# A hybrid attention layer: half-height score products tied into runs, the linear attention's levels taken two at a time

## The chip, the cores and the metric

One core of one Trainium2 chip runs the whole layer. The metric is the device time of one execution in microseconds (us), lower is better. The core has TensorE (products, with weights loaded ahead of them), VectorE, ScalarE, GpSimd and SyncE (which issues most of the transfers).

## What is computed

One layer over 256 latent tokens and 256 context tokens, width 2048, in float32. The part that the change touches:

```python
h = modulate(rms_norm(x, norm1_w), shift, scale)              # for latents and context
gq, gk, gv, gr, gaf, gab, dq, dk, dv = split(h @ w_in)
# linear attention, 8 heads of 64 (q, k) and 128 (v), forwards and backwards, with decays:
scores = einsum('bhid,bhjd,bhijd->bhij', qc, kc, exp(b_i - b_j))   # b: running sum of log decays
o = scores @ v + (q * exp(b)) @ state
# differential attention, 8 heads, two maps of 64 each, 256 queries, 512 keys:
q, k = rope(rms_norm(q)), rope(rms_norm(k))                   # k of the context without rope
p = softmax(q @ k.T * 64 ** -0.5)
o = (p[0] - lam * p[1]) @ v
# then: norms of o, gates, projections, output projection, gated MLP with a width-3 convolution
```

## The kernel before

The tokens lie in the free dimension, channels on the 128 partitions. Weights come from HBM in tiles of 512 KB, are split into a high and a low part (`split`: ScalarE copies to fp32r, L206; VectorE or GpSimd subtracts, L213), and each weights' product is made of two or three fp32r products over these parts (`col_tile` L262/L264, `row_tile` L275 to L277, `both_tile` L311 to L313). These products are the bulk of the time; the two attentions run between them.

The program is given to a planner that orders each engine's instructions by their priority and by its own simulated times; tiles of one tag share buffers, and a tile waits for a free one. Inside `high_priority(500)` an instruction goes ahead of the weights' products as soon as the planner thinks that its operands are there. `after(later, earlier)` ties two instructions of one engine in that order, without a wait. In PSUM there are four accumulator banks (`acc_bank`) and four auxiliary ones: two of the kind aux0, two of aux1 (`aux_bank(name, j)`).

The linear attention works on four pairs of heads (`gla_pair`), each pair's two heads on partitions 0 to 63 and 64 to 127. A pair makes its decays' running sums (`bfb`), the state from the context (key transposes L777, state products L782, both in aux0 banks), and then scores for two chunks of 128 tokens: one set for q and k as they are (`score(q, kl, ...)`), one off-diagonal set between the chunks, and one set for each of seven levels (`LEVELS`, spans of 64 down to 1). A level's factors `e` (two buffers) are four subtractions on GpSimd (L832 to L835), an exponential on ScalarE (L836) and a product with q and k on VectorE (L837). A set of scores is four f32 products of 64 rows (`score`, L808): two chunks, and in each the two heads, head j into a bank of kind aux j. Each bank is then copied into `at`: with a mask by VectorE for a level (L839), by ScalarE for the other two sets (L815, L822). At the end the outputs take two state products of 64 rows per head (L845) and two with values (L848).

The differential attention (`scores`, `attend`) takes 8 heads and two blocks of 128 queries. One `scores(h, c)` makes six fp32r products of 64 rows and 512 columns (L965): for each of the two maps m, on partitions m*64 to m*64+63 and into a bank of kind aux m, query high by key high, query low by key high, query high by key low. Per head the kind aux0 holds `s` twice, one `pT`, `o` and `oss`; the kind aux1 holds `s` twice and one `pT`. `halves` makes the high and low parts (high on ScalarE first, low on VectorE from it). The gates' products (`gate_tile`) and the projections (`pga`, `pgb`) follow.

The norms' sums (`sums`, 24 of them, in `heads_norm` and `onormed`) multiply a matrix of ones by the high and the low part of the squares (L594, L595).

Of the kernel before, what the change touches and what calls it, by code (L numbers as in the profile page):

```python
# [9 lines left out]
F32 = mybir.dt.float32  # L10
# [8 lines left out]
P = 128  # L19
D = 2048  # L20
T = 256
# [125 lines left out]
def layer_kernel(tc, I, out):  # L147
# [3 lines left out]
    with es:  # L151
# [438 lines left out]
        def sums(o, m, sq, halves=None):  # L590

            n = sq.shape[1]
            hi, lo = halves or split(sq, n)
            PE.matmul(o, m, hi[:, :n], start=True, stop=False)  # L594
            PE.matmul(o, m, lo[:, :n], start=False, stop=True)  # L595
# [77 lines left out]
        with tc.tile_pool(name="gla", bufs=1) as pg:  # L673
# [60 lines left out]
            def gla_pair(p):  # L734
# [67 lines left out]
                def score(Q, K, off, take):  # L802

                    bs = [aux_bank("sc", j) for j in range(2)]
                    for c in range(2):
                        cq = 1 - c if off else c
                        for j in range(2):
                            PE.matmul(bs[j][:, c * P:(c + 1) * P], K[j * 64:(j + 1) * 64, c * P:(c + 1) * P],  # L808
                                      Q[j * 64:(j + 1) * 64, cq * P:(cq + 1) * P], start=True, stop=True)
# [5 lines left out]
                score(q, kl, False, lambda v, b: S.activation(v, b, AF.Copy, scale=2.0))  # L815
                e = pg.tile([P, 2, T], F32, tag="e", bufs=2, name="e")
                S.activation(e[:, 0, P:], bfb[:, 0, P:], AF.Exp, scale=1.0 / 16)
                S.activation(e[:, 0, :P], bfb[:, 1, :P], AF.Exp, scale=1.0 / 16)
                S.activation(e[:, 1, :P], bfb[:, 0, :P], AF.Exp, scale=-1.0 / 16, bias=bl[:, 0:1])
                S.activation(e[:, 1, P:], bfb[:, 1, P:], AF.Exp, scale=-1.0 / 16, bias=bl[:, 1:2])  # L820
                V.tensor_tensor(e, e, qk[p][:, 0:2, :], op=ALU.mult)
                score(e[:, 0, :], e[:, 1, :], True, lambda v, b: S.copy(v, b))  # L822
                for li, m in enumerate(LEVELS):
                    e = pg.tile([P, 2, T], F32, tag="e", bufs=2, name="e")
                    g = T // (2 * m)
                    f4 = bfb[:, 0, :].rearrange("p (g h m) -> p g h m", h=2, m=m)
                    b4 = bfb[:, 1, :].rearrange("p (g h m) -> p g h m", h=2, m=m)
                    q4 = e[:, 0, :].rearrange("p (g h m) -> p g h m", h=2, m=m)
                    k4 = e[:, 1, :].rearrange("p (g h m) -> p g h m", h=2, m=m)
                    fm = f4[:, :, 0, m - 1:m].to_broadcast([P, g, m])  # L830
                    bm = b4[:, :, 1, 0:1].to_broadcast([P, g, m])
                    G.tensor_tensor(q4[:, :, 1, :], f4[:, :, 1, :], fm, op=ALU.subtract)  # L832
                    G.tensor_tensor(q4[:, :, 0, :], b4[:, :, 0, :], bm, op=ALU.subtract)
                    G.tensor_tensor(k4[:, :, 0, :], fm, f4[:, :, 0, :], op=ALU.subtract)
                    G.tensor_tensor(k4[:, :, 1, :], bm, b4[:, :, 1, :], op=ALU.subtract)  # L835
                    S.activation(e, e, AF.Exp, scale=1.0 / 16)  # L836
                    V.tensor_tensor(e, e, qk[p][:, 0:2, :], op=ALU.mult)  # L837
                    mk = masks[:, li:li + 1, :].to_broadcast([P, 2, P])
                    score(e[:, 0, :], e[:, 1, :], False, lambda v, b: V.copy_predicated(v, mk, b))  # L839
# [68 lines left out]
        with tc.tile_pool(name="diff", bufs=1) as pd:  # L908
# [49 lines left out]
            def scores(h, c):  # L958
# [3 lines left out]
                for i, j in ((0, 0), (1, 0), (0, 1)):  # L962
                    for m in range(2):
                        r = slice(m * 64, (m + 1) * 64)
                        PE.matmul(bs[m], qs[h][r, i, c * P:(c + 1) * P], ks[h][j][r, :], start=i + j == 0, stop=j == 1)  # L965
# [258 lines left out]
```

## Time and profile before

| | us |
|---|---|
| median of 3 runs | 1749.18 (1746.83 to 1751.12) |
| the profiled execution | 1749.72 |
| its span, first to last instruction | 1747.9 |
| TensorE busy | 1715.5 (98%), 10460 products |
| VectorE, ScalarE, GpSimd busy | 1230.4, 981.4, 491.8 |

The span lies inside the profiled execution's time; starts in the trace count from the span's start. In the trace's rows "L808 MATMUL sc<-e 64*128 64x128" is an instruction of line 808 that writes tile sc from tile e, with 64 rows and 128 columns of the array, and 64 partitions by 128 elements of moving operand. Neighbours of one line are merged (x8), and a merged row has the first one's start and the time to the last one's end; ends of products are modelled, starts are recorded. A bracket gives the idle time of the engine ahead of the row, and what ended it.

### The profile page before, as it was taken

The page shows a single profiled execution, that of the slowest core. Times are in us where ns is not written, and L with a number is a line of the kernel's source. Part 1 is how long each engine was busy: PE and PEld are TensorE (multiplying, and loading weights), DVE is VectorE, ACT ScalarE, POOL GpSimd, SP SyncE. Part 2 cuts the span into 40 slices and gives each one's busy share as a digit, 9 for nine tenths or more (in the row PEclk, how much of TensorE's full clock was granted, in tenths as well). Part 3 has the DMA queues.
Part 4 walks back from the last instruction along what each step waited for, and adds up shares of the span by engine and source line. Part 5 has one row for each costly group of instructions (what it writes and reads, how often), then busy time and mean ns, then how long its engine had stood idle before and what let it go on. Part 6 is the DMA issues. An engine that isn't in the chain of part 4 may idle for free. (4 is left out here: it accounts for less than half of the span.)

```text
span 1747.9 us, 29267 instructions
## 1 busy us (share of the span) xinstructions
PE 1715.5 (98%) x10460; PEld 1473.6 (84%) x10460; DVE 1230.4 (70%) x2230; ACT 981.4 (56%) x1980; POOL 491.8 (28%) x474
## 2 busy tenths in 40 slices
PE   8999999999999999999999999999999999999999
PEld 5779999988877788887878898888888888888888
DVE  4555756778687787767876888777877877644443
ACT  5335455664345776744655676666666666544443
POOL 0002534646121222223353422222222222222222
PEclk9999999999999999999999999999999999999999
DMA  9995532435766354588666656666766666666664
GB/s 384 408 402 173 163 116 75 133 109 182 247 198 202 123 168 160 187 263 313 224 222 219 192 187 212 223 227 229 233 224 228 225 224 225 209 194 202 196 199 139
DMA packets 108451, 368.75 MB, mean 211 GB/s; under 512 B 12176, under 2 KB 17040, under 8 KB 108304
## 3 DMA queue, kind: packets, MB, share of 16 engines
q1 hardware_dynamic: 103264, 362.51, 62.1%
q10 hardware_dynamic: 5040, 4.37, 0.8%
q8 instruction: 82, 1.34, 0.3%
q14 instruction: 65, 0.53, 0.1%
HBM read 364.73 MB, written 2.10 MB: 210 GB/s over the span
## 5 line engine op out<-in xcount | busy, mean ns | idle before, releaser
L206 ACT CAST whi<-wraw 128x512 fp32r<-128x512 f32 (+2 forms) x1004 | 603.1, 608 | 384.9 <-PE down L262 109.4
L213 DVE TENSOR_TENSOR wlo<-wraw,whi 128x512 fp32r<-128x512 f32 (+2 forms) x761 | 539.2, 716 | 258.5 <-ACT whi L206 253.6
L213 POOL TENSOR_TENSOR wlo<-wraw,whi 128x512 fp32r<-128x512 f32 (+2 forms) x243 | 337.3, 1388 | 948.1 <-ACT whi L206 845.8
L262 PE MATMUL down<-g,whi 128*128 128x512 f32 x704 | 243.6, 392 | 0.0
L262 PE MATMUL upg<-a,whi 128*128 128x512 f32 x656 | 229.6, 392 | 0.0
L262 PE MATMUL upv<-a,whi 128*128 128x512 f32 x656 | 229.5, 392 | 0.0
L336 DVE CUSTOM_DVE_ANT_0 araw<-araw,cb 128x1024 f32<-128x1024 f32 x128 | 173.6, 1359 | 33.9 <-DMA araw<-in_w_ada 33.9
L264 PE MATMUL down<-g,wlo 128*128 128x256 f32 x704 | 195.4, 280 | 0.7 <-DVE wlo L213 0.7
L264 PE MATMUL upg<-a,wlo 128*128 128x256 f32 x656 | 183.0, 280 | 1.1 <-DVE wlo L213 1.1
L264 PE MATMUL upv<-a,wlo 128*128 128x256 f32 x656 | 183.1, 280 | 0.6 <-DVE wlo L213 0.5
L262 PE MATMUL gate<-a,whi 128*128 128x512 f32 x512 | 180.6, 397 | 0.0
L262 PEld LDWEIGHTS down<-g,whi 128*128 128x128 f32 x704 | 131.0, 187 | 28.3
L262 PEld LDWEIGHTS upv<-a,whi 128*128 128x128 f32 x656 | 122.4, 187 | 26.9
L262 PEld LDWEIGHTS upg<-a,whi 128*128 128x128 f32 x656 | 122.4, 187 | 26.8
L264 PE MATMUL gate<-a,wlo 128*128 128x256 f32 x512 | 139.8, 283 | 3.0 <-DVE wlo L213 3.0
L264 PEld LDWEIGHTS down<-g,wlo 128*128 128x128 f32 x704 | 132.9, 189 | 1.9 <-DVE wlo L213 1.0
L264 PEld LDWEIGHTS upg<-a,wlo 128*128 128x128 f32 x656 | 123.9, 189 | 2.5 <-DVE wlo L213 2.0
L264 PEld LDWEIGHTS upv<-a,wlo 128*128 128x128 f32 x656 | 123.9, 189 | 1.8 <-DVE wlo L213 1.2
L262 PEld LDWEIGHTS gate<-a,whi 128*128 128x128 f32 x512 | 94.4, 188 | 21.0 <-issue 2.3
L264 PEld LDWEIGHTS gate<-a,wlo 128*128 128x128 f32 x512 | 96.4, 188 | 9.4 <-DVE wlo L213 4.6
L262 PE MATMUL mix<-a,whi 128*128 128x512 f32 x256 | 89.1, 396 | 0.8 <-ACT whi L206 0.8
L264 PE MATMUL mix<-a,wlo 128*128 128x256 f32 x256 | 69.3, 282 | 1.9 <-POOL wlo L213 1.3
(332 smaller groups left out, 3408.7 us busy)
## 6 DMA issues: line engine op xcount, KB each, us to landing
wraw<-in_w_up SPq DMA_DIRECT2D x164, 512.0 KB, 4.3
araw<-in_w_ada SPq DMA_DIRECT2D x128, 512.0 KB, 4.7
wraw<-in_w_down SPq DMA_DIRECT2D x80, 512.0 KB, 3.8
ada<-in_w_ad SPq DMA_DIRECT2D x64, 512.0 KB, 10.0
wraw<-in_w_gate SPq DMA_DIRECT2D x64, 512.0 KB, 4.2
wraw<-in_w_in SPq DMA_DIRECT2D x58, 512.0 KB, 4.1
wraw<-in_w_proj SPq DMA_DIRECT2D x32, 512.0 KB, 4.6
wraw<-in_w_out SPq DMA_DIRECT2D x32, 512.0 KB, 4.1
```

Of the source, the lines that this page charges most:

```text
L206: copied[0] = S.copy(hi[:, :n], raw)
L213: i = e.tensor_tensor(lo[:, :n], raw, hi[:, :n].bitcast(F32), op=ALU.subtract)
L262: i = PE.matmul(b.rearrange("p (a b) -> p a b", a=2), whi[:, sl], acts[k], start=first, stop=last)
L264: i = PE.matmul(b[:, T:], wlo[:, sl], acts[k][:, 1, :], start=False, stop=last)
L336: i = V.tensor_tensor_reduce(raw, raw, cb[:, q * 1024:(q + 1) * 1024], 1.0, 0.0, op0=ALU.mult, op1=ALU.add, accum_out=ada2[:, j, q:q + 1])
```

## The change

Three edits, all of them of order.

In `sums` the low part's product comes first and the high part's is tied behind it. In `scores` of the differential attention the six products start with the one that needs the key's low part, the two maps in turn, and each is tied behind the one before. In `gla_pair` the products within a set of scores are tied in their order; the off-diagonal set now comes first, with the set of q and k tied behind it; and the levels' factors are made for two levels, whereupon both sets of scores follow in one tied run, the later level in front. What is computed by each instruction is the same.

```diff
--- before.py
+++ after.py
@@ -591,8 +591,8 @@
 
             n = sq.shape[1]
             hi, lo = halves or split(sq, n)
-            PE.matmul(o, m, hi[:, :n], start=True, stop=False)
-            PE.matmul(o, m, lo[:, :n], start=False, stop=True)
+            i = PE.matmul(o, m, lo[:, :n], start=True, stop=False)
+            after(PE.matmul(o, m, hi[:, :n], start=False, stop=True), i)
 
         def heads_norm(b, wname, done, o, sq, y):
 
@@ -799,44 +799,59 @@
                 at = pg.tile([P, 2, 2, T], F32, tag="at", name="at")
 
 
-                def score(Q, K, off, take):
+                def score(Q, K, off, take, run):
+
 
                     bs = [aux_bank("sc", j) for j in range(2)]
                     for c in range(2):
                         cq = 1 - c if off else c
                         for j in range(2):
-                            PE.matmul(bs[j][:, c * P:(c + 1) * P], K[j * 64:(j + 1) * 64, c * P:(c + 1) * P],
-                                      Q[j * 64:(j + 1) * 64, cq * P:(cq + 1) * P], start=True, stop=True)
+                            i = PE.matmul(bs[j][:, c * P:(c + 1) * P], K[j * 64:(j + 1) * 64, c * P:(c + 1) * P],
+                                          Q[j * 64:(j + 1) * 64, cq * P:(cq + 1) * P], start=True, stop=True)
+                            if run:
+                                after(i, run[-1])
+                            run.append(i)
                     for j in range(2):
                         v = at[:, j].rearrange("p c i -> p (c i)")
                         v = v[:, P:3 * P] if off else v.rearrange("p (a b) -> p a b", b=P)[:, 0:4:3, :]
                         take(v, bs[j][:, :T] if off else bs[j][:, :T].rearrange("p (a b) -> p a b", b=P))
 
-                score(q, kl, False, lambda v, b: S.activation(v, b, AF.Copy, scale=2.0))
-                e = pg.tile([P, 2, T], F32, tag="e", bufs=2, name="e")
-                S.activation(e[:, 0, P:], bfb[:, 0, P:], AF.Exp, scale=1.0 / 16)
-                S.activation(e[:, 0, :P], bfb[:, 1, :P], AF.Exp, scale=1.0 / 16)
-                S.activation(e[:, 1, :P], bfb[:, 0, :P], AF.Exp, scale=-1.0 / 16, bias=bl[:, 0:1])
-                S.activation(e[:, 1, P:], bfb[:, 1, P:], AF.Exp, scale=-1.0 / 16, bias=bl[:, 1:2])
-                V.tensor_tensor(e, e, qk[p][:, 0:2, :], op=ALU.mult)
-                score(e[:, 0, :], e[:, 1, :], True, lambda v, b: S.copy(v, b))
-                for li, m in enumerate(LEVELS):
+                def factors(li):
+
                     e = pg.tile([P, 2, T], F32, tag="e", bufs=2, name="e")
-                    g = T // (2 * m)
-                    f4 = bfb[:, 0, :].rearrange("p (g h m) -> p g h m", h=2, m=m)
-                    b4 = bfb[:, 1, :].rearrange("p (g h m) -> p g h m", h=2, m=m)
-                    q4 = e[:, 0, :].rearrange("p (g h m) -> p g h m", h=2, m=m)
-                    k4 = e[:, 1, :].rearrange("p (g h m) -> p g h m", h=2, m=m)
-                    fm = f4[:, :, 0, m - 1:m].to_broadcast([P, g, m])
-                    bm = b4[:, :, 1, 0:1].to_broadcast([P, g, m])
-                    G.tensor_tensor(q4[:, :, 1, :], f4[:, :, 1, :], fm, op=ALU.subtract)
-                    G.tensor_tensor(q4[:, :, 0, :], b4[:, :, 0, :], bm, op=ALU.subtract)
-                    G.tensor_tensor(k4[:, :, 0, :], fm, f4[:, :, 0, :], op=ALU.subtract)
-                    G.tensor_tensor(k4[:, :, 1, :], bm, b4[:, :, 1, :], op=ALU.subtract)
-                    S.activation(e, e, AF.Exp, scale=1.0 / 16)
+                    if li is None:
+                        S.activation(e[:, 0, P:], bfb[:, 0, P:], AF.Exp, scale=1.0 / 16)
+                        S.activation(e[:, 0, :P], bfb[:, 1, :P], AF.Exp, scale=1.0 / 16)
+                        S.activation(e[:, 1, :P], bfb[:, 0, :P], AF.Exp, scale=-1.0 / 16, bias=bl[:, 0:1])
+                        S.activation(e[:, 1, P:], bfb[:, 1, P:], AF.Exp, scale=-1.0 / 16, bias=bl[:, 1:2])
+                    else:
+                        m = LEVELS[li]
+                        g = T // (2 * m)
+                        f4 = bfb[:, 0, :].rearrange("p (g h m) -> p g h m", h=2, m=m)
+                        b4 = bfb[:, 1, :].rearrange("p (g h m) -> p g h m", h=2, m=m)
+                        q4 = e[:, 0, :].rearrange("p (g h m) -> p g h m", h=2, m=m)
+                        k4 = e[:, 1, :].rearrange("p (g h m) -> p g h m", h=2, m=m)
+                        fm = f4[:, :, 0, m - 1:m].to_broadcast([P, g, m])
+                        bm = b4[:, :, 1, 0:1].to_broadcast([P, g, m])
+                        G.tensor_tensor(q4[:, :, 1, :], f4[:, :, 1, :], fm, op=ALU.subtract)
+                        G.tensor_tensor(q4[:, :, 0, :], b4[:, :, 0, :], bm, op=ALU.subtract)
+                        G.tensor_tensor(k4[:, :, 0, :], fm, f4[:, :, 0, :], op=ALU.subtract)
+                        G.tensor_tensor(k4[:, :, 1, :], bm, b4[:, :, 1, :], op=ALU.subtract)
+                        S.activation(e, e, AF.Exp, scale=1.0 / 16)
                     V.tensor_tensor(e, e, qk[p][:, 0:2, :], op=ALU.mult)
-                    mk = masks[:, li:li + 1, :].to_broadcast([P, 2, P])
-                    score(e[:, 0, :], e[:, 1, :], False, lambda v, b: V.copy_predicated(v, mk, b))
+                    return e
+
+
+
+                e, run = factors(None), []
+                score(e[:, 0, :], e[:, 1, :], True, lambda v, b: S.copy(v, b), run)
+                score(q, kl, False, lambda v, b: S.activation(v, b, AF.Copy, scale=2.0), run)
+                for first in range(0, len(LEVELS), 2):
+                    es = [(li, factors(li)) for li in range(first, min(first + 2, len(LEVELS)))]
+                    run = []
+                    for li, e in es[::-1]:
+                        mk = masks[:, li:li + 1, :].to_broadcast([P, 2, P])
+                        score(e[:, 0, :], e[:, 1, :], False, lambda v, b: V.copy_predicated(v, mk, b), run)
 
                 obs = [aux_bank("o", j) for j in range(2)]
                 for j in range(2):
@@ -959,10 +974,15 @@
 
                 pm = []
                 bs = [aux_bank("s", m) for m in range(2)]
-                for i, j in ((0, 0), (1, 0), (0, 1)):
+                last = None
+                for i, j in ((0, 1), (0, 0), (1, 0)):
                     for m in range(2):
                         r = slice(m * 64, (m + 1) * 64)
-                        PE.matmul(bs[m], qs[h][r, i, c * P:(c + 1) * P], ks[h][j][r, :], start=i + j == 0, stop=j == 1)
+                        mm = PE.matmul(bs[m], qs[h][r, i, c * P:(c + 1) * P], ks[h][j][r, :], start=j == 1,
+                                       stop=i == 1)
+                        if last is not None:
+                            after(mm, last)
+                        last = mm
                 sm = pd.tile([P, 4], F32, tag="sm", bufs=3, name="sm")
                 for m in range(2):
                     V.tensor_reduce(sm[:, m:m + 1], bs[m], axis=AX.X, op=ALU.max)
```

## Rows read from the trace of the kernel before

**Rows 1.** Busy us and instructions in two stretches: PE, PEld, DVE, ACT, POOL; then clock, DMA.
```profile
150.00:440.00 290.00, 287.20 (x2056) 259.25 (x2056) 201.79 (x350) 161.49 (x346) 136.21 (x169) 1.00 0.41 135
...
505.00:720.00 215.00, 211.52 (x1064) 166.66 (x1064) 163.43 (x339) 136.59 (x297) 46.53 (x36) 0.99 0.51 169
```

**Rows 2.** TensorE's waits, 150 to 440 us: total us, times, longest us.
```profile
PE sc L808 <- DVE e L837: 0.9, 2, 0.7
```

**Rows 3.** TensorE's timeline around one piece: start us, us, instruction, count.
```profile
191.63 0.29 PE L277 MATMUL gvb<-wlo,c 128*128 128x272 f32 x1
191.76 0.29 PE L275 MATMUL gvb<-whi,c 128*128 128x272 f32 x1
191.97 1.16 PE L808 MATMUL sc<-e 64*128 64x128 f32 x8
193.06 0.40 PE L276 MATMUL gvb<-whi,c 128*128 128x272 f32 x1
193.29 0.29 PE L277 MATMUL gvb<-wlo,c 128*128 128x272 f32 x1
```

**Rows 4.** TensorE's timeline, pair of heads 1, two sets of scores.
```profile
267.51 0.28 PE L312 MATMUL gk<-c,whi 128*128 128x256 f32 x1
267.72 0.71 PE L808 MATMUL sc<-e 64*128 64x128 f32 x8
268.36 0.39 PE L313 MATMUL gk<-c,wlo 128*128 128x256 f32 x1
...
269.87 0.71 PE L808 MATMUL sc<-e 64*128 64x128 f32 x8
```

**Rows 5.** TensorE's timeline, pair of heads 0, two levels together.
```profile
206.25 0.29 PE L277 MATMUL gvb<-wlo,a 128*128 128x272 f32 x1
206.47 1.16 PE L808 MATMUL sc<-e 64*128 64x128 f32 x16
207.56 0.39 PE L275 MATMUL gvb<-whi,c 128*128 128x272 f32 x1
```

**Rows 6.** TensorE's timeline around the last softmax scores.
```profile
699.64 0.28 PE L264 MATMUL gate<-a,wlo 128*128 128x256 f32 x1
699.76 0.39 PE L262 MATMUL gate<-a,whi 128*128 128x512 f32 x1
700.08 0.96 PE L965 MATMUL s<-ks,qs 64*128 64x512 f32 x3
700.97 0.38 PE L264 MATMUL gate<-a,wlo 128*128 128x256 f32 x1
```

**Rows 7.** TensorE's timeline around four softmax scores.
```profile
512.71 0.39 PE L277 MATMUL dvb<-wlo,c 128*128 128x512 f32 x1
512.93 0.39 PE L275 MATMUL dvb<-whi,c 128*128 128x512 f32 x1
513.25 0.74 PE L965 MATMUL s<-ks,qs 64*128 64x512 f32 x4
513.92 0.50 PE L276 MATMUL dvb<-whi,c 128*128 128x512 f32 x1
```

**Rows 8.** TensorE's timeline: first, third and last 64-row piece of the linear attention (of 41).
```profile
150.68 0.71 PE L808 MATMUL sc<-qk 64*128 64x128 f32 x4
...
188.38 0.71 PE L808 MATMUL sc<-qk 64*128 64x128 f32 x4
...
436.03 1.41 PE L845 MATMUL o<-qe,state 64*128 64x256 f32 x8
```

**Rows 9.** TensorE's timeline: first piece of softmax scores (of 36).
```profile
507.88 1.21 PE L965 MATMUL s<-ks,qs 64*128 64x512 f32 x8
```

**Rows 10.** GpSimd's timeline: next factors after a released buffer.
```profile
268.55 0.43 POOL L832 TENSOR_TENSOR e<-bfb 128x128 f32<-128x128 f32 x1 [3.07 <-PE sc L808]
```

**Rows 11.** ScalarE's timeline: the first values copied out.
```profile
472.32 1.27 ACT L937 COPY dv<-dvb 128x512 f32<-128x512 f32 x2 [0.28 <-PE dvb L277]
```

**Rows 12.** The projections' first products, by tile: ns min/median/max, first and last start.
```profile
L262 PE MATMUL pga<-ya,whi x128: 388/396/400, 812.1 to 907.4; 128*128 128x512 f32 x128
```

## The prediction

> **What bounds the kernel now.** I read the stretches first. While the linear attention runs beside the projections (150 to 440 us) TensorE is busy 287.20 of 290 us, and while the softmax attention runs (505 to 720 us) 211.52 of 215 us; VectorE, the next, has 201.79 and 163.43 us [rows 1]. So in both stages that the change touches the end is set by the TensorE time of the products, provided that their operands come. Then I read what TensorE waits for: in the linear attention the longest total at a score product is 0.9 us, in two waits for a factor [rows 2]. There is little waiting to remove. What remains is the price of each product, and that is in the timeline.
>
> A product of scores uses 64 rows, half of TensorE's height; the weights' products use 128. Call a piece the 64-row products between two others. I read its price from the start of the product ahead of it to the start of the product behind it, less the ordinary slot of the one ahead, plus 0.1 us, since the slot of the one behind is longer too (193.06 to 193.29, where 191.63 to 191.76 is an ordinary one, 0.125 [rows 3]). Ordinary slots are 0.12 us at 256 columns [rows 6] and 0.22 at 512 [rows 7]. An f32 product appears as two instructions, so a set of four products is x8.
>
> - Eight instructions on one half of the rows: 191.76 to 193.06 is 1.30, so 1.28 us [rows 3].
> - Eight that alternate the halves: 267.51 to 268.36 is 0.85, so 0.83 us [rows 4]. Count and shapes are the same; the halves overlap.
> - Sixteen alternating, two sets in one piece: 206.25 to 207.56 is 1.31, so 1.29 us [rows 5], not 2 x 0.83. The 0.39 us between (0.4 with rounding) are what one more piece costs.
> - Softmax scores, three on one half: 699.76 to 700.97 is 1.21, so 1.09 us [rows 6]. Four that alternate: 512.93 to 513.92 is 0.99, so 0.87 us [rows 7].
>
> **The linear attention.** Between 150.68 and 436.03 us I count 41 pieces, the outputs' state products included [rows 8]. By length: 14 of eight alternating (0.84 each), 6 of eight on one half (1.29), 9 of four (0.84), 4 of sixteen (1.29), 3 of two and one of six (together 3.5), two of state products (2.8), two of sixteen that end in state products (1.81 each), and 1.5 us of real waits (another 0.6 sits in the 3.5). Sum 43.6 us. One-sided pieces come from banks: the first head pair's products of q and k are split, x4 at 150.68 and x4 at 188.38 [rows 8], one half long before its sister.
>
> After: the off-diagonal set stands in front of q and k, both tied; the seven levels come as 2+2+2+1. At best a pair of heads has one piece for the first two sets (1.29), three for levels (1.29 each), and the last level with the state products (1.81): 6.97 us. Where the first two sets still part, 2 x 0.84 instead of 1.29 gives 7.36; I take this, because the key transposes and the state products take a bank of the same kind just ahead in the code. Four pairs: 29.5 us, a gain of 14.1. Upper bound: 15.7, if they do not part.
>
> Lower bound: two levels in one run want all four auxiliary banks at once, and the 38 us between the halves at 150.68 and 188.38 show a product held for a bank. The Trainium skill has this as a rule (TensorEngine Tiling (Array Packing), Gotcha 1: PSUM Pressure): row tiles need different banks, so row tiling raises the demand for them. By it no two levels would join, and a pair of heads would cost 8.5 us instead of 7.36. From the rows: 12 joints at 0.39 are 4.7 us, so the gain is 9.4. I stay with 14.1, since [rows 5] shows two whole sets in one piece, with all four banks, before anything was tied.
>
> **The softmax scores.** Between 507.88 and 700.08 us the 96 products lie in 36 pieces [rows 6, 9]: 16 of three on one half (17.4), 6 of one (0.73 each), 9 of two (7 at 0.93, 2 at 0.61), 4 of four (3 at 0.87, one 1.3), one of eight (2.1, of it 0.8 waiting). Sum 35.5 us. The code's order alternates the halves already, but one half's bank comes free first, and its three go ahead. The change ties the six, half 0 in front. Its kind of bank has five users per head in the code, the other's three, so half 0 is usually the late one; when it can start, its sister can. Six alternating in one piece: 0.87 for four and 0.24 for two more side by side, 1.11 us. Sixteen of them: 17.8, a gain of 17.7. If five still split in two, at 0.37 each, 15.9; I take that. Lower bound: nothing, if the half in front is the early one.
>
> **The norms' sums.** 24 sums now take the low part first, with the high part tied behind. Both are 128-row products of one length, so no piece and no slot changes: 0. The low part was the last operand before as well. At worst each sum is ready one slot later, 0.12 to 0.22 us, hidden under weights' products.
>
> **The chain through the levels.** Two levels at a time means that the factors' two buffers come back together. Before, GpSimd stood 3.07 us and began the next factors at 268.55 [rows 10], released by the score set at 267.72; the other buffer's set came at 269.87 [rows 4]. Waiting for both adds about 2.2 us, plus 0.4 for the longer run, and there are now three such turns per pair of heads: 4 x 3 x 2.6 = 31 us at most. Against it, the off-diagonal set no longer waits behind q and k (188.38 [rows 8]; its second half went at 191.97 [rows 3]), 3 us per pair: 19 us net, and I allow 0 to 31. No product of the stage needs these outputs: they begin at 436.03 [rows 8], and the next stage's first values are copied at 472.32 [rows 11]. That leaves 36 us, less the 14 by which the stream ahead of the copy gets shorter, 22. In the softmax stage the early half waits for its sister, which delays its exponentials by some 1.5 us in each of 16 turns, 24 us; the last scores go at 700.08 [rows 6], the projections that need the results begin at 812.1 [rows 12]. Both are hidden. Where that cover is gone, each further microsecond of chain is one of TensorE idle: at 31 us, 9.
>
> **The sum.** 14.1 + 15.9 = 30.0 us. Off it: the real waits in the pieces (1.5 + 0.6 + 0.8) I expect to come back elsewhere, 2.9. And a faster TensorE meets its suppliers more often: VectorE has 76% of the softmax stage already [rows 1]. I take off 4 us for that and for the new order's own waits, an estimate between 0 and 10 (10 would be 0.15 us for each of 28 + 16 + 24 runs). Net 23.1 us. The profiled execution has 1749.72 us beside its span of 1747.9, 0.5 us over the median: 1749.7 - 23.1 = 1726.6.
>
> **Rivals.**
> (a) Half of it. A tie fixes the order among the tied; it does not keep other products out. If the levels do not join (9.4) and half of the softmax gain stays away (8), 17.4 less 7 leaves 10: 1740. For it: sums already stand between scores, and all four banks are wanted. Against it: [rows 5].
> (b) No change. The banks set the order as before, and what is saved goes to operands that are late: 1745 to 1754. Against it: in the linear attention whole levels already alternate wherever both operands are there [rows 4, 5], and a tied run does not start until its last operand is there.
> (c) Slower. TensorE takes its queue in order. A run now has its latest operand in front, and where the written order expects it too early, everything behind it waits. There are 68 runs; to eat 27 us the mean new wait must exceed 0.4 us; at 0.5 it is 34, and the time 1757. For it: two products did wait 0.9 us for a factor [rows 2]. Against it: that is 0.02 us for each of the 41 pieces. The Trainium skill's page TensorE: Matmul & The Clock Gate (The mechanism) has the rule that products are strictly first in, first out; by it each such wait is paid in full, 34 us here. No row before shows a long one.
>
> **Chances.** Forecast 0.63 (1718 to 1734), (a) 0.20 (1734 to 1744), (b) 0.09, (c) 0.08. A change of less than 0.3%, 5 us, can't be told from none here. The lower end 1717 is both upper bounds together (15.7 + 17.7) with nearly nothing lost; the upper end 1741 takes in (a). Faster 0.83, same 0.09, slower 0.08.
>
> **What would show it.** 64-row pieces of the linear attention down from 41 to 24 to 28, three of them per pair of heads x16 at 1.29 us, and no one-sided x4 or x8. Softmax pieces down from 36 to 16 to 21, most of them x6 at 1.1 us. The way from 150 us to the first softmax score shorter by some 12 us, from there to the first projection by some 14. GpSimd's factors in bursts of two levels with longer gaps. The prediction is wrong if the pieces stay near 41 and 36, if TensorE's waits for factors, sums and keys' low parts rise above some 15 us, or if the weights' low parts on VectorE come late throughout the softmax stage.

## The result, and the profile after

The changed kernel takes 1731.26 us (median of 4 runs, 1730.35 to 1734.49) against 1748.66 for the kernel before on the same chip: a ratio of 0.9905 [0.9891, 0.9920], 17.4 us faster. Its profiled execution has 1731.72 us, with a span of 1729.9.

The profile's page: busy us, share of the span and instructions of each engine.

```profile
span 1729.9 us, 29264 instructions
...
PE 1690.9 (98%) x10460; PEld 1464.9 (85%) x10460; DVE 1227.8 (71%) x2230; ACT 977.4 (56%) x1980; POOL 481.0 (28%) x474
```

TensorE has as many products as before and is busy 24.6 us less (1715.5 before), while the span is only 18.0 us shorter (1747.9 before). So more was saved than arrived. The two stretches of [rows 1], in the kernel after:

```profile
150.00:440.00 290.00, 283.44 (x2076) 258.29 (x2074) 202.79 (x354) 160.97 (x347) 134.08 (x170) 0.99 0.42 139
...
505.00:720.00 215.00, 211.15 (x1164) 175.37 (x1163) 174.23 (x353) 143.43 (x314) 47.29 (x39) 1.00 0.56 187
```

In the linear attention TensorE is now busy 283.44 us where it had 287.20: 3.8 us of new idle time. In the softmax stage its busy time is the same, but with 1164 instructions in it instead of 1064, and VectorE is up from 163.43 to 174.23.

Then the pieces, on TensorE's timeline: a run of two levels, the last level with the state products, the first softmax scores and a later six of them.

```profile
193.13 0.29 PE L277 MATMUL gvb<-wlo,a 128*128 128x272 f32 x1
193.35 1.16 PE L809 MATMUL sc<-e 64*128 64x128 f32 x16
194.44 0.39 PE L275 MATMUL gvb<-whi,a 128*128 128x272 f32 x1
...
438.55 0.71 PE L809 MATMUL sc<-e 64*128 64x128 f32 x8
439.10 1.13 PE L860 MATMUL o<-qe,state 64*128 64x256 f32 x8
...
514.10 1.67 PE L981 MATMUL s<-ks,qs 64*128 64x512 f32 x12
...
597.57 0.28 PE L595 MATMUL oss<-osqs,ones 128*128 128x256 f32 x1
597.78 0.98 PE L981 MATMUL s<-ks,qs 64*128 64x512 f32 x6
598.69 0.50 PE L262 MATMUL gate<-a,whi 128*128 128x512 f32 x1
```

Sixteen at 193.35 answer to [rows 5] and cost the same (1.31 less the slot and plus 0.1, as the prediction reads it). Six at 597.78 answer to [rows 6, 7]: 597.57 to 598.69 is 1.12, less 0.12 and plus 0.1 is 1.10 us, where three on one half cost 1.09. The row before the six is a norm's high part: a sum now stands ahead of the scores, not between them. I priced all the pieces so, and put down as a stall what any other product's slot has over its ordinary length, from 0.04 us on:

| | before | after |
|---|---|---|
| pieces of the linear attention | 41, 43.6 us | 26, 32.2 us (1.8 of it waits) |
| pieces of the softmax scores | 36, 35.5 us | 15, 17.1 us |
| stalls, first gv product to first dvb | 4.0 us | 12.5 us |
| stalls, first dvb to first softmax score | 3.7 us | 8.0 us |
| stalls, first score to first pga | 10.6 us | 11.4 us |
| of the stalls, in stretches at half clock | 1, 1.6 us | 3, 4.9 us |
| first gv product to first pga | 665.7 us | 648.2 us |
| from there to the last product | 931.8 us | 930.4 us |

The pieces give back 11.4 + 18.4 = 29.8 us. The stalls of the three stretches take 31.9 - 18.3 = 13.6 of it. That leaves 16.2; the stretch is 17.5 shorter, and the difference lies in slots too small to be listed. How much counts as stall depends on what is taken as a product's ordinary slot: with the median slot of each line of code, the three rows are up to 4 us higher in both columns, and their sum grows by 10.6 us. From the pieces and the stretch alone, 29.8 less 17.5, it is 12.3. Of the 13.6 us of new stalls 12.8 lie ahead of the first softmax score. TensorE's waits there (146 to 515 us; total us, times, longest), where before had 0.9 us as its longest total [rows 2]:

```profile
PE o L863 <- DVE at L854: 2.1, 1, 2.1
PE dvb L277 <- DVE wlo L213: 1.5, 1, 1.5
PE hss L594 <- DVE rc L756: 1.3, 1, 1.3
PE hss L594 <- DVE wlo L213: 1.3, 1, 1.3
PE kT L777 <- POOL rc L772: 1.3, 2, 0.6
PE sc L809 <- DVE e L841: 1.2, 1, 1.2
PE gr L264 <- DVE wlo L213: 1.1, 2, 1.0
```

No single one is long; most wait for VectorE, which has 70% of the stage. Two of the places, before and after (the windows' columns as above):

```profile
318.00:328.00 10.00, 10.00 (x69) 8.81 (x68) 6.61 (x13) 5.11 (x12) 6.57 (x5) 1.00 0.20 64
388.00:398.00 10.00, 9.38 (x63) 8.21 (x63) 7.77 (x12) 6.12 (x13) 5.77 (x5) 1.00 0.16 56
```

```profile
318.00:328.00 10.00, 8.03 (x38) 6.07 (x37) 9.54 (x13) 7.42 (x17) 5.97 (x7) 0.83 0.30 90
388.00:398.00 10.00, 7.08 (x28) 5.10 (x26) 9.64 (x12) 6.34 (x13) 4.44 (x3) 0.83 0.27 71
```

VectorE is busy 9.54 and 9.64 of 10 us where it had 6.61 and 7.77, and TensorE's granted clock, 1.00 before, is 0.83: a stretch of 3.4 us at its lower level (1.2 of 2.4 GHz) begins at 321.7 and at 393.4, each time just after TensorE has stood 2 to 3 us in two or three waits. TensorE's timeline at the first place:

```profile
319.23 0.66 PE L777 MATMUL kT<-ident,rc 128*128 128x128 f32 x4 [0.63 <-POOL rc L772]
319.64 0.48 PE L262 MATMUL gr<-a,whi 128*128 128x512 f32 x1
321.46 0.57 PE L594 MATMUL hss<-wlo,bones 128*128 128x512 f32 x1 [1.34 <-DVE rc L756]
```

**The chains.** GpSimd's factors start at 263.35 and 271.66, one burst for two levels (its timeline; [rows 10] before), and the first values are copied at 471.65 (ScalarE's; 472.32 in [rows 11]).

```profile
263.35 0.77 POOL L836 TENSOR_TENSOR e<-bfb 128x128 f32<-128x128 f32 x1 [4.84 <-PE sc L809]
...
271.66 0.64 POOL L836 TENSOR_TENSOR e<-bfb 128x128 f32<-128x128 f32 x1 [0.90 <-PE sc L809]
```

```profile
471.65 1.95 ACT L952 COPY dv<-dvb 128x512 f32<-128x512 f32 x3 [0.28 <-PE dvb L277]
```

The first softmax score starts at 514.10, later than before (507.88, [rows 9]), though the stream ahead is shorter. From the first dvb product to there, the tile dvb gets 246 products instead of 224: weights' products moved ahead of the first run, and their 22 slots of 0.23 us are 5 us. That is a shift of order and no loss. The projections' first product is at 795.5 (812.1 in [rows 12]).

### The profile page after: what moved, and what is told of

Read it like the earlier page. It is cut to its first block, busy times and chain, and to the rows that moved or that the text cites. A ratio compares the mean times of both kernels' runs of the same rounds, so it can differ in the third digit from the quotient of the medians.

```text
span 1729.9 us, 29264 instructions
## 1 busy us (share of the span) xinstructions
PE 1690.9 (98%) x10460; PEld 1464.9 (85%) x10460; DVE 1227.8 (71%) x2230; ACT 977.4 (56%) x1980; POOL 481.0 (28%) x474
## 5 line engine op out<-in xcount | busy, mean ns | idle before, releaser
L213 DVE TENSOR_TENSOR wlo<-wraw,whi 128x512 fp32r<-128x512 f32 (+2 forms) x761 | 529.7, 704 | 246.9 <-ACT whi L206 242.3
L213 POOL TENSOR_TENSOR wlo<-wraw,whi 128x512 fp32r<-128x512 f32 (+2 forms) x243 | 330.6, 1361 | 944.1 <-ACT whi L206 845.2
L336 DVE CUSTOM_DVE_ANT_0 araw<-araw,cb 128x1024 f32<-128x1024 f32 x128 | 180.7, 1415 | 33.9 <-DMA araw<-in_w_ada 33.6
```

What stands on the lines that cost most here:

```text
L213: i = e.tensor_tensor(lo[:, :n], raw, hi[:, :n].bitcast(F32), op=ALU.subtract)
L336: i = V.tensor_tensor_reduce(raw, raw, cb[:, q * 1024:(q + 1) * 1024], 1.0, 0.0, op0=ALU.mult, op1=ALU.add, accum_out=ada2[:, j, q:q + 1])
```

## The experiments

Each ratio is to the kernel before, run on the same chip; the changed kernel has 0.9905 [0.9891, 0.9920]. The intervals reach 2 to 5 us to either side, so smaller differences between versions are not told apart by time, only by the pieces and stalls read from the traces. Each trace is of one execution. In the cuts of code, which show the main lines, "..." stands for lines left out.

**1. The norms' sums put back**, the rest as changed:

```diff
-            i = PE.matmul(o, m, lo[:, :n], start=True, stop=False)
-            after(PE.matmul(o, m, hi[:, :n], start=False, stop=True), i)
+            PE.matmul(o, m, hi[:, :n], start=True, stop=False)
+            PE.matmul(o, m, lo[:, :n], start=False, stop=True)
```

> The changed kernel with the norms' sums as before (high part first, not tied). Theory A: the low part in front makes TensorE wait for VectorE at two sums, 1.3 us each, and a lower clock follows each; without it 5 to 6 us come back, so about 1725.5 us against 1731.3. Rival B: the new waits belong to the other two edits and to the new order as such; then the time stays at 1731 within 2 us, with other products waiting in the same places. The 64-row pieces stay at 26 and 15 by both.

Measured: 1739.96 us, 0.9951 [0.9933, 0.9968], 8.7 us slower than the changed kernel (8.0 by the ratios). Neither theory had this: one expected a gain, the other no change, and both 26 and 15 pieces. The softmax pieces go from 15 to 22 (17.1 to 24.4 us), those of the linear attention from 32.2 to 33.9 us. TensorE's timeline shows how:

```profile
550.15 0.73 PE L981 MATMUL s<-ks,qs 64*128 64x512 f32 x3 [1.24 <-DVE oraw L622]
551.08 0.39 PE L595 MATMUL oss<-osqs,ones 128*128 128x256 f32 x1 [0.20 <-DVE osqs L232]
551.40 1.16 PE L981 MATMUL s<-ks,qs 64*128 64x512 f32 x3
```

The second product of a sum, which takes the low part and is tied to nothing here, lands inside six tied scores. With the low part in front, both products of a sum come when the later operand is there, and stand side by side.

**2. The softmax edit alone** (to the kernel before):

```diff
-                for i, j in ((0, 0), (1, 0), (0, 1)):
+                last = None
+                for i, j in ((0, 1), (0, 0), (1, 0)):
                     for m in range(2):
...
+                        if last is not None:
+                            after(mm, last)
+                        last = mm
```

> The kernel before with only the six softmax scores tied. Theory A (price of pieces): pieces in the softmax stage 36 to about 16, their cost 35.5 to about 17.5 us, so 18 us less, of which up to 4 go to new waits: 1731 to 1735 us. Rival B (a tie alone moves nothing, it is the levels' order that frees the banks): 30 pieces or more stay, gain under 9 us, 1740 or more.

Measured: 1739.15 us, 0.9942 [0.9923, 0.9961]. 22 softmax pieces of 23.8 us, 11.7 less than before; stalls as before (3.8, 5.4 and 9.3 us). That lies between the two theories. The tie works by itself, but six of the 16 runs are split, here as in experiment 1, and all six by a sum's second product (L595).

**3. The linear attention's edit alone** (`gla_pair` as changed, `sums` and `scores` as before):

```diff
-            i = PE.matmul(o, m, lo[:, :n], start=True, stop=False)
-            after(PE.matmul(o, m, hi[:, :n], start=False, stop=True), i)
+            PE.matmul(o, m, hi[:, :n], start=True, stop=False)
+            PE.matmul(o, m, lo[:, :n], start=False, stop=True)
...
-                for i, j in ((0, 1), (0, 0), (1, 0)):
+                for i, j in ((0, 0), (1, 0), (0, 1)):
...
```

> The kernel before with only the linear attention's edit (ties, off-diagonal set first, two levels at a time). Theory A: 41 pieces become about 26, 43.6 us become about 31, so 12 us less; with the waits for the last outputs (2 us) and little else 1738 to 1741 us. Rival B: this edit brings most of the new waits (13 us in the changed kernel); then the gain is under 5 us, 1744 or more.

Measured: 1751.40 us, 1.0015 [1.0004, 1.0027]: no gain at all, as Rival B had it. The pieces are fewer as planned, 25 with 30.7 us, 12.9 saved. The stalls ahead of the first score went from 7.7 to 23.1 us, and four stretches at half clock cost 6.5 of it.

**4. The norms' sums alone** (the first two removed and added lines of the change):

```diff
-            PE.matmul(o, m, hi[:, :n], start=True, stop=False)
-            PE.matmul(o, m, lo[:, :n], start=False, stop=True)
+            i = PE.matmul(o, m, lo[:, :n], start=True, stop=False)
+            after(PE.matmul(o, m, hi[:, :n], start=False, stop=True), i)
```

> The kernel before with only the norms' sums turned and tied. Theory A: the products cost the same, the low part in front waits for VectorE while it makes the running sums, 2 to 6 us with the lower clock behind it: 1751 to 1755 us. Rival B: nothing, since the low part was the last operand before as well: 1747 to 1750 us.

Measured: 1745.25 us, 0.9979 [0.9970, 0.9988]: 3.7 us faster. The softmax pieces fall from 36 to 30 (35.5 to 30.9 us), although nothing in `scores` was touched. The prediction had put this edit at nothing, and both theories had 1747 us or more.

**5. Sums and softmax without the linear attention's edit:**

```diff
-                            i = PE.matmul(bs[j][:, c * P:(c + 1) * P], K[j * 64:(j + 1) * 64, c * P:(c + 1) * P],
-                                          Q[j * 64:(j + 1) * 64, cq * P:(cq + 1) * P], start=True, stop=True)
-                            if run:
-                                after(i, run[-1])
-                            run.append(i)
+                            PE.matmul(bs[j][:, c * P:(c + 1) * P], K[j * 64:(j + 1) * 64, c * P:(c + 1) * P],
+                                      Q[j * 64:(j + 1) * 64, cq * P:(cq + 1) * P], start=True, stop=True)
...
-                for first in range(0, len(LEVELS), 2):
...
+                for li, m in enumerate(LEVELS):
...
```

> Sums and softmax scores as changed, the linear attention as before. Theory A: the 11 us that the linear attention's pieces save are paid back as late operands and lower clock (levels alone: 12.9 saved, time 2 us longer), so without this edit the time is that of the changed kernel within 3 us, 1728 to 1734, with 41 to 43 pieces at about 44 us and late operands until the values' products at about 4. Rival B: the edit pays when the other two are there; then 1737 to 1742.

Measured: 1736.76 us, 0.9933 [0.9913, 0.9953], close to Rival B; 43 and 15 pieces, 44.4 and 17.1 us; stalls before the first dvb 4.1 us, and no stretch at half clock. In the stretch from 150 to 440 us (windows) TensorE is as busy as before (287.20, [rows 1]):

```profile
150.00:440.00 290.00, 287.15 (x2057) 258.59 (x2057) 202.38 (x351) 161.87 (x347) 135.27 (x169) 1.00 0.41 134
```

So the linear attention's edit is worth some 5.5 us beside the other two (1736.76 less 1731.26, 4.9 by the ratios; their intervals overlap by 0.0007, so the time alone does not make this sure), and alone it costs 2.6. The parts seem not to add: by their ratios at 1749 us softmax, linear attention and sums alone give -10.1, +2.6 and -3.7, in sum -11.2, and together -16.6. That difference, 5.4 us, is hardly more than the uncertainty of the four ratios. The pieces do add: 11.7, 12.9 and 4.6 us alone are 29.2, against 29.8 together.

**6. The levels one at a time**, tied within a set, off-diagonal set in front:

```diff
-                for first in range(0, len(LEVELS), 2):
-                    es = [(li, factors(li)) for li in range(first, min(first + 2, len(LEVELS)))]
+                for first in range(len(LEVELS)):
+                    es = [(li, factors(li)) for li in range(first, first + 1)]
```

> The changed kernel with the levels one at a time instead of two, ties and the off-diagonal set in front kept. Theory A: seven level pieces instead of four for each pair of heads, 3 x 0.39 x 4 = 4.7 us more for products; if the waits of the linear attention (12.5 us of late operands until the values' products, 4.0 before) come from taking two levels together, up to 8 us come back and the time is 1727 to 1730. Rival B: the waits come from the off-diagonal set in front, or from the order as such; then the time is 1734 to 1737.

Measured: 1735.68 us, 0.9929 [0.9902, 0.9956]. 32 pieces, 32.6 us, hardly more than with two levels together (32.2): six more pieces at 0.39 would be 2.3 us, and the 1.8 us of waits inside the changed kernel's pieces are gone. The time is that of Rival B. The stalls before the first dvb are the largest of all, 16.5 us, in other places (TensorE's waits):

```profile
PE dk L313 <- DVE rc L756: 3.8, 1, 3.8
PE gq L264 <- DVE wlo L213: 2.7, 1, 2.7
```

**7. Only the ties within a set**, with the order of before (q and k first, one level after the other):

```diff
-                def score(Q, K, off, take, run):
-
+                def score(Q, K, off, take):
+                    run = []
...
-                for first in range(0, len(LEVELS), 2):
...
+                for li, m in enumerate(LEVELS):
...
```

> Sums and softmax scores as changed; in the linear attention only the four products of one set tied, sets in the order of before and levels one at a time. Theory A: one-sided pieces go (12 of them and the split first sets), about 5 us of the 44 are saved without the levels' waits: 1725 to 1729. Rival B: any new order of the linear attention brings late operands: 1731 or more.

Measured: 1730.99 us, 0.9902 [0.9883, 0.9922], the same as the changed kernel, and as Rival B had it. 32 pieces, 33.0 us; stalls 12.1, 6.0 and 10.4 us. The four ties of a set bring nearly all that the edit brings; the set in front and the levels two at a time add 0.8 us of pieces and nothing that the time shows. The stalls are there too.

**8. The halves apart:** the run has three products of half 0 and then three of half 1.

```diff
-                for i, j in ((0, 1), (0, 0), (1, 0)):
-                    for m in range(2):
+                for m in range(2):
+                    for i, j in ((0, 1), (0, 0), (1, 0)):
```

> The changed kernel with the six softmax scores still one tied run, but three on one half of the rows and then three on the other. Theory A (two gains, fewer pieces and the overlap of the halves): one piece per run stays, but only one pair in it overlaps, so a piece of six costs some 1.6 to 1.8 us instead of 1.09; over 16 runs 8 to 11 us, 1739 to 1742. Rival B (only the number of pieces counts): 1731 within 2.

Measured: 1734.06 us, 0.9916 [0.9894, 0.9937], 2.8 us slower than the changed kernel, inside the uncertainty. The 8 to 11 us that theory A gave for halves that don't overlap did not come:

```profile
595.32 0.28 PE L595 MATMUL oss<-osqs,ones 128*128 128x256 f32 x1
595.53 0.97 PE L981 MATMUL s<-ks,qs 64*128 64x512 f32 x6
596.43 0.51 PE L264 MATMUL dq<-a,wlo 128*128 128x256 f32 x2
```

From 595.32 to 596.43 are 1.11 us, so this piece costs 1.09, as when the halves alternate, although the queue has them three and three. The 16 pieces cost 21.3 us, mainly because three have waits behind them (at 531, 569 and 600 us) and one is split; the profiled execution, 1738.33 us, is the slowest of the four. So this is not Rival B's count of pieces alone: the halves overlap here too.

**9. Half 1 in front**, alternating:

```diff
-                    for m in range(2):
+                    for m in (1, 0):
```

> The changed kernel with half 1 of the rows in front of half 0 in each run of softmax scores. Theory A (half 1 has the bank that comes free first): half 1's first product goes ahead alone and the other five follow when half 0 has its bank, so 24 to 32 pieces instead of 15, 4 to 6 us more for them: 1735 to 1738. Rival B (both banks are there at about the same time, the tie alone does it): 15 to 17 pieces, 1731 within 2.

Measured: 1737.74 us, 0.9939 [0.9924, 0.9954], as theory A had it. 28 pieces, 25.4 us: 12 of one, 14 of five, one of two and one of twelve.

```profile
592.42 0.49 PE L981 MATMUL s<-ks,qs 64*128 64x512 f32 x1
...
597.26 0.96 PE L981 MATMUL s<-ks,qs 64*128 64x512 f32 x5
```

The first product, of half 1, goes alone, and the other five, with one of half 0 in front, follow 4.8 us later. So half 0 is the late one, as the prediction took it, and the product in front has to be the one that can go last. That the cause is its bank fits, since both halves read the same tiles otherwise, but no row names it.

**10. Two of GpSimd's products to VectorE.** GpSimd's rows at 317.88 and 319.12 stand beside VectorE's long ones in the changed kernel (below, under the hardware), and TensorE waits for both engines there. If they were the cause, moving them would take the waits away.

```diff
-                G.tensor_tensor(rc, rc, qk[p][:, 2:3, :].to_broadcast([P, 2, T]), op=ALU.mult)
+                V.tensor_tensor(rc, rc, qk[p][:, 2:3, :].to_broadcast([P, 2, T]), op=ALU.mult)
...
-                G.tensor_tensor(qe, qe, qk[p][:, 0:1, :].to_broadcast([P, 2, T]), op=ALU.mult)
+                V.tensor_tensor(qe, qe, qk[p][:, 0:1, :].to_broadcast([P, 2, T]), op=ALU.mult)
```

> The changed kernel with two products of each pair of heads (decays by k, decays by q) on VectorE instead of GpSimd. Theory A (the linear attention's new waits are VectorE's subtractions running beside GpSimd's products, 1.76 us instead of 0.68, and the key transposes behind GpSimd): the waits at 318 to 321 and 388 to 392 us and the lower clock behind them go, stalls until the values' products fall from 12.5 to 6 us or less, time 1724 to 1727. Rival B (any new order has some such waits): 1730 to 1734, the waits stand in other places.

Measured: 1732.44 us, 0.9909 [0.9894, 0.9924], as Rival B had it. No stretch at half clock is left, but the stalls before the first dvb are still 12.3 us. The waits went elsewhere (TensorE's waits, 146 to 515 us):

```profile
PE dvb L277 <- DVE wlo L213: 3.1, 2, 1.7
PE dk L313 <- DVE wlo L213: 1.7, 1, 1.7
PE gr L264 <- POOL wlo L213: 1.6, 2, 1.2
```

**11. Both:** the ties within sets (7) and the two products on VectorE (10).

```diff
-                def score(Q, K, off, take, run):
+                def score(Q, K, off, take):
+                    run = []
...
-                G.tensor_tensor(rc, rc, qk[p][:, 2:3, :].to_broadcast([P, 2, T]), op=ALU.mult)
+                V.tensor_tensor(rc, rc, qk[p][:, 2:3, :].to_broadcast([P, 2, T]), op=ALU.mult)
...
```

> Sums and softmax scores as changed, the four products of a set tied and nothing else of the levels' edit, and the two products on VectorE. Theory A: 1731 less 5 to 6 us for the waits, 1724 to 1727. Rival B: 1730 to 1734.

Measured: 1732.31 us, 0.9911 [0.9894, 0.9928]; stalls 9.4, 6.5 and 12.0 us, pieces 34.3 and 17.2. No gain over either.

**12. VectorE relieved:** 17 of its products for the conditioning (L336, 1.2 us each) moved from the linear attention's stretch to the gates.

```diff
-GATE_ADA = [0.25] * 24 + [2] * 8
+GATE_ADA = [0.98] * 24 + [2] * 8
...
-                    ada_next(0.5)
...
-                ada_next(0.5)
...
-                ada_next(1)
...
-                ada_next(0.5)
...
-                ada_next(0.25)
```

> The changed kernel with the 17 conditioning dots of the linear attention's stretch (1.22 us each on VectorE, 21 us of its 203 there) put into the gates' stretch. Theory A (a TensorE that is 11 us faster is late for VectorE's low parts, and VectorE's load is what makes them late): stalls between the first values of the linear attention and the first product of the next stage's values fall from 12.5 to 7 us or less, that stretch ends earlier, and the whole is 1726 to 1731, something being lost again in the gates. Rival B (the written order expects operands too early whatever VectorE carries): the stalls stay at 11 to 14 us, and the time is 1731 to 1736.

Measured: 1736.74 us, 0.9935 [0.9918, 0.9952], some 5 us slower than the changed kernel (the intervals touch). VectorE's busy time in the stretch (third column behind the window's length) did fall, by 18.8 us:

```profile
150.00:440.00 290.00, 283.68 (x2082) 258.75 (x2081) 184.04 (x319) 161.25 (x348) 127.61 (x170) 0.99 0.34 113
```

TensorE gained nothing from it (283.68 busy against 283.44); the stalls before the first dvb are 13.5 us, against 12.5, as Rival B had them. The stage that took the products on has 16.8 us of stalls instead of 11.4. A mean load of VectorE that is 9% lower takes away none of TensorE's stalls in the linear attention.

## Why the prediction was right, and which steps of it were not

The forecast was 1726.6 us in a range of 1717 to 1741, faster with a chance of 0.83; it came to 1731.3. The mechanism is shown: the products take less time when the 64-row ones stand in fewer pieces with both halves together. They saved 29.8 us where the sum had 30.0, but that the two agree so closely is partly luck: the composition is another.

Two effects lie in the 29.8, and no run parts them. By the prediction's 0.39 us for one more piece, 15 and 21 fewer pieces are 5.9 and 8.2 us, 14 in all (an estimate). Most of the rest comes from halves that now run side by side: three products on one half cost 1.09 us, and six on both cost 1.10. (The two rows that the prediction names for 0.39 give 2 x 0.83 less 1.29, 0.37; with the 0.84 of other such pieces it is 0.39.)

- **Linear attention: 14.1 forecast, 11.4 measured.** The pieces are 26, as said (24 to 28). Ten runs of x16 cost 1.29 as forecast, four end in state products at 1.81, and the rest are ten of eight, one of ten and one of six. The first two sets part in every pair of heads, as the sum had it; beyond that two pairs of levels were parted, and 1.8 us of waits lie inside pieces. Rival (a)'s claim that the four banks keep levels from joining fell: ten of twelve joints happened. What the Trainium skill states (TensorEngine Tiling (Array Packing), Gotcha 1: PSUM Pressure) is that row tiles write to different banks; that two levels would therefore not join was the prediction's inference, and these pieces contradict it. Joining is worth little, though: experiment 7, with levels joined only where they happened to meet, is as fast.
- **Softmax: 15.9 forecast, 18.4 measured.** Fourteen runs of six at 1.09 us (1.11 forecast) and one of twelve; none of the five splits that I had allowed for, without a reason. With the six tied in this order, splits come only without the sums' edit (22 pieces in experiments 1 and 2), and the timeline of experiment 1 shows a sum's product inside the six. The kernel before shows it already: five of its six pieces of one stand right behind a sum's second product.
- **The norms' sums: 0 forecast, 4.6 to 7.3 us of pieces measured** (experiments 4 and 1), 3.7 and 8.7 us in the time. This step failed. I had asked whether the sums' own slots change. I had not asked where the second product of a sum lands when it waits alone: among the 64-row products, where it costs a piece. Rival (a) did say that sums already stand between scores, but no price was put on it, and the splits of the runs were put down to banks. In the kernel before (TensorE's timeline):

```profile
550.64 0.73 PE L965 MATMUL s<-ks,qs 64*128 64x512 f32 x2
551.30 0.39 PE L595 MATMUL oss<-osqs,ones 128*128 128x256 f32 x1
551.62 0.50 PE L965 MATMUL s<-ks,qs 64*128 64x512 f32 x1
```

  Alone, the softmax edit saves 11.7 us of pieces and not 15.9, and the sums bring 6.7 more on top (experiments 2 and 5), so the two errors nearly cancel in the total.
- **The chain of levels: hidden, as forecast**, but for 2.1 us (`o` at L863 waiting for `at`). The copy at 471.65 against 472.32 shows it. The sister's delay in the softmax chain is hidden too: from the first score to the first pga 281.4 us against 304.2, 23 us less where 14 was said: 18.4 us of pieces, and some 5 us of weights' products that moved ahead of the first score. For the same reason "150 us to the first softmax score shorter by 12" was wrong in place: it became 6 us longer.
- **The waits: 2.9 + 4 forecast, some 13.6 measured**, of it 3.3 us more at half clock. This is the term that was mis-sized, and it holds nearly the whole miss: 6.7 us, where the time was 4.7 above the forecast. It is about the upper end of my estimate (2.9 + 10), and so it is with the 12.3 that the pieces and the stretch alone give.
- **Rival (c)** had the right mechanism for part of it: experiment 3 loses all its 12.9 us of pieces to stalls. But its place, the front of the 68 runs, holds only a part of them: one score product and two sums' low parts, 3.8 of the 11.4 us of waits ahead of the first score (the list above and three smaller entries). And one of the two sums' waits (for `rc`, 1.3 us) stays when the sums are put back: it moves to the second product (experiment 1). The rest are `o`, key transposes and weights' products, most of these with low parts. By the Trainium skill's rule of products strictly first in, first out (TensorE: Matmul & The Clock Gate, The mechanism) such a wait is paid in full wherever it is; the waits here agree with that as far as idle rows of 0.6 to 2.1 us on TensorE's timeline show it.

What makes the new stalls is settled only in part. Shown: they come with fewer pieces of the linear attention. Every version that saves these has 9.4 to 16.5 us of stalls before the first dvb, in places that differ from version to version; every version that does not (before, experiments 2, 4, 5) has 3.8 to 4.4. They do not need the two-level runs (7), nor GpSimd's two products (10, 11), nor the last 9% of VectorE's mean load (12). A burst of VectorE work is not enough by itself either: in experiment 7 VectorE is busy 9.82 us of the first place, and TensorE stands nowhere in it:

```profile
318.00:328.00 10.00, 10.00 (x65) 8.66 (x64) 9.82 (x13) 8.29 (x16) 5.22 (x4) 1.00 0.33 102
```

Argued only: TensorE arrives earlier at operands that the other engines deliver at a pace of their own, and stands where the operand that it needs next is behind a burst. What in the written order brings the two together stays open; a version with VectorE's work spread around 318 and 388 us was not tried.

## What to carry to other kernels

Price half-height products by the transitions to and from them (here 0.37 to 0.39 us for one more piece) and by whether both halves run side by side, not by their number. So look at what stands between them, and tie a run with the operand in front that comes last. A lone product of another kind that waits for its own operand is what splits runs, so order those products too. On a stream that is 98% busy, price what you save, and expect a part of it back as waits in new places (here 13.6 of 29.8 us). Compare the suppliers' load before and after in windows of 10 us: a mean of 70% hides places at 95%, though such a place did not always make TensorE wait.

## What the runs showed of the hardware that was not expected

**The two halves overlap even when the queue has one half's three products first.** In experiment 8 the six products of a piece start at 595.532, 595.542, 595.869, 595.879, 596.098 and 596.108 us, in pairs 10 ns apart, nearly as in the changed kernel (597.782, 597.785, 598.120, 598.124, ...). The end signals, which in the queue stand on the third and the sixth, are recorded on the fifth and the sixth. That the queue holds them three and three shows in the same signals: in all 13 pieces of six of experiment 8 both add more than one, in the 14 of the changed kernel one of the two adds one. So a product of half 1 started ahead of two products of half 0 that were queued before it. The Trainium skill says that products start and end strictly in program order (TensorE: Matmul & The Clock Gate, The mechanism); for two row halves this trace differs, and the measurement decides.

**VectorE's products with two inputs take turns with GpSimd's.** The factors' product takes 0.68 us alone and up to 1.74 here, a low part's subtraction of the same size 1.76, in the changed kernel (VectorE's timeline, then GpSimd's):

```profile
206.36 0.68 DVE L841 TENSOR_TENSOR e<-e,qk 128x512 f32<-128x512 f32 x1
...
318.42 1.30 DVE L841 TENSOR_TENSOR e<-e,qk 128x512 f32<-128x512 f32 x1 [1.71 <-ACT e L826]
319.64 1.76 DVE L213 TENSOR_TENSOR wlo<-nsq,whi 128x512 fp32r<-128x512 f32 x1
321.34 1.74 DVE L841 TENSOR_TENSOR e<-e,qk 128x512 f32<-128x512 f32 x1
```

```profile
317.88 1.29 POOL L772 TENSOR_TENSOR rc<-rc,qk 128x512 f32<-128x512 f32 x1 [0.66 <-ACT rc L771]
319.12 1.73 POOL L797 TENSOR_TENSOR qe<-qe,qk 128x512 f32<-128x512 f32 x1
320.81 1.73 POOL L213 TENSOR_TENSOR wlo<-wraw,whi 128x512 fp32r<-128x512 f32 x1
```

GpSimd's end at 319.17, 320.85 and 322.54; VectorE's end at 319.72, 321.40 and 323.08, each 0.54 to 0.55 us later, though it had started well before. That agrees with the Trainium skill (SBUF — State Buffer, SBUF: two separate sides), which has a VectorE instruction with two SBUF inputs and a GpSimd instruction that reads SBUF lock each other out, each for the whole instruction. Three such turns in a row cost VectorE 2.8 us (4.80 less 3 x 0.68) just where TensorE waits; experiment 10 shows that removing them there is not enough.
